# Fill up to 4200 columns a tick, and unread products behind the fill, in a hybrid decoder layer on one core

## The chip, the cores and the metric

The kernel runs on one core of one Trainium2 chip. The metric is the device time of one execution in microseconds (us). Below, PE is TensorE's matmul side and PEld its weight load, DVE is VectorE, ACT is ScalarE, POOL is GpSimd and SP is SyncE, which here issues most of the DMAs.

## The reference, cut to what matters

One layer of a decoder with two SwiGLU blocks and, between them, four mixers that read one combined projection. It is computed for 1024 prompt tokens and for 8 x 4 sample tokens; both go through the projections together, as 1056 columns.

```
h = x + 0.5 * rms_norm(swiglu(rms_norm(x, ng[0]), ...), ng[1])
cols = rms_norm(h, ng[2]) @ p['w_in']
c_gla, c_gmlp, c_rwkv, c_dil = split_at(cols, [GLA_COLS, GMLP_COLS, RWKV_COLS, DIL_COLS])
...
mix = jnp.concatenate([o_gla, o_gmlp, o_rwkv, o_dil], axis=-1) @ p['w_out']
h = h + rms_norm(mix, ng[3])
h = h + 0.5 * rms_norm(swiglu(rms_norm(h, ng[4]), ...), ng[5])
```

The mixers are gated linear attention (gla), a spatial gating (gmlp), RWKV-7 (rwkv) and dilated attention with three groups (dil). Their outputs are long chains of small products and elementwise steps. The products with `w_in`, `w_out` and the SwiGLU weights are large.

## The kernel before, in words

**Large products.** A matrix and its input are each split into two parts of type fp32r, and three products (high times high, high times low, low times high) replace one fp32 product. A product with `w_in` writes a tile `pw` of 128 x 352 (lines 139, 142 and 143, eight times for one tile). The products of the first half of `w_out` (channels of gmlp, rwkv: K3) write `pz`, 128 x 256 (line 2897), and a copy on ScalarE (line 2911) takes each `pz` to the sum `z`. The second half of `w_out` (gla and dil: K4) needs the last mixers; its products (line 204) open what is called the head here: the end of the layer's middle and the start of the second SwiGLU.

**Weights.** `load(j)` brings 512 KB of weights by a DMA of SP (`wraw`), `part(j)` splits them with a cast on ScalarE (line 111, `whi`) and a subtraction on GpSimd (line 112, `wlo`). Both calls stand inside the fill below, so they move with it.

**Two kinds of work in one order.** The program is recorded once, and within it a class `Loom` decides in which order steps are recorded. An engine runs its instructions in that order. The *fill* is one generator, `line()`: the rest of the first SwiGLU, the products with `w_in`, those of K3, a mark `"end"`, and behind `L.mixed == 3` the head. The *streams* are generators of the mixers with priorities. A step runs up to a `yield`. `Loom` keeps rough clocks of all engines from costs of its own (`cost`, `note`), among them the time at which TensorE is free, `free[pe]`, and the columns that went through TensorE (`flow`; `ticks` by stretches of 3.4133 us on that rough clock).

**The rule.** `run` records a step of the fill whenever TensorE is thought to have had little to do, and a step of a stream otherwise:

```
return now > TICK and (sum(n for _, n in self.flow) < WARM or self.ticks.get(k - 1, 0) < FULL)
...
if others and self.cool() and self.weft():
    continue
```

`cool` (line 1446) holds when fewer than `WARM` = 3000 columns lie in the last 3.4133 us of the rough clock, or fewer than `FULL` = 3060 in the last whole stretch. `weft` (line 1531) records one step of the fill: six products of `pw`, or six of `pz`. It returns False when the fill waits for something or is used up. If no stream can go on either, the rough clock is moved ahead.

**The stages that matter below.** The rwkv mixer and gmlp come first, then gla and dil run side by side (dil's attention: lines 2065, 2096, 2107; its merge of the groups: line 2206; its sample tokens: lines 2313 to 2358, with the cached values `cv` loaded by 36 DMAs; gla: lines 2514 to 2616). After the mixers, `mixes01` loads gla's output again (`mx`) and splits it, and only then is `L.mixed` set to 3, which lets the fill go on with the head. From `"end"` to there the fill has nothing to give.

Of the kernel before, what the change touches and what calls it, by code (L numbers as in the profile page):

```python
# [11 lines left out]
F32 = mybir.dt.float32  # L12
# [16 lines left out]
NF = 22  # L29
DF = (0,)  # L30
AGE = 3.
WARM = 3000
I2 = 10.
V, S, G = "vector", "scalar", "gpsimd"
KA = (V, G)
# [15 lines left out]
class Layer:  # L51
    def __init__(self, ctx, tc, I, O):
        self.ctx, self.tc, self.nc = ctx, tc, tc.nc
        self.I, self.O = I, O
        self.pace = Pace()
        self.room = {}
        self.const = ctx.enter_context(tc.tile_pool(name="const", bufs=1))
# [908 lines left out]
class Pace:  # L966
# [11 lines left out]
    def run(self, h):  # L978
        try:
            h[0] = max(h[0], self.clock) + (next(h[1]) or 0.0)  # L980
        except StopIteration:
            h[1] = None
            self.tasks.remove(h)
# [415 lines left out]
class Loom:  # L1399
# [4 lines left out]
    def __init__(self, tc, fill):  # L1404
        self.tc, self.ins = tc, tc.nc.cur_bb.bb.instructions
        self.i, self.last = len(self.ins), {}
        self.free, self.wrote, self.used, self.slots, self.red = {}, {}, {}, {}, {}
        self.fill, self.done, self.over = fill, {}, False
        self.live, self.hold, self.due = [], None, 0.0
        self.fresh, self.marks = [], []  # L1410
        self.ticks, self.flow, self.cells = {}, [], [0.0] * 16
        self.pe = tc.nc.tensor.engine
        self.kept = ()

    def keep(self, engines):

        self.kept = [getattr(self.tc.nc, e).engine for e in engines]
# [27 lines left out]
    def cool(self):  # L1445
# [4 lines left out]
        k = int(now / TICK)  # L1450
        return now > TICK and (sum(n for _, n in self.flow) < WARM or self.ticks.get(k - 1, 0) < FULL)

# [62 lines left out]
    def after(self, gen, prio):  # L1515

        self.fresh.append(self.add(gen, prio))
# [12 lines left out]
    def weft(self):  # L1530
# [13 lines left out]
        self.done[v] = self.late  # L1544
        return True

    def got(self, names):

        return all(self.done.get(n, 1e9) <= self.free.get(self.pe, 0.0) for n in names)
# [24 lines left out]
    def run(self, until, others=True):  # L1574

        while not until():
            now = self.free.get(self.pe, 0.0)
            if others and self.cool() and self.weft():
                continue
            ok = [s for s in self.live if others and self.open(s, now)]  # L1580
            go = [s for s in ok if s[2] <= now + SLACK]
            if go:
                self.step(min(go, key=lambda s: s[0] - (now - s[2]) / AGE))
            elif not self.weft():
                self.free[self.pe] = min(t for t in [self.due] + [s[2] for s in ok] + list(self.done.values()) if t > now)
                self.cells = [max(t, self.free[self.pe]) for t in self.cells]

    def all(self, streams):
        self.run(lambda: all(s[1] is None for s in streams))
# [296 lines left out]
def last_rows(L, ap, raw):  # L1886

    nc, O = L.nc, L.O
    yield lambda: L.loom.got(RW)
    last = ap.tile([128, 8, 33], F32, name="last", tag="mV")  # L1890
    L.dma(last, raw[:, :, TP - 1:T].rearrange("j p t -> p j t"))
    yield
    for jh in range(2):
        rows = ap.tile([33, 512], F32, name="lrows", tag="mvn")
        q = L.ps.tile([128, 512], F32, name="pm", tag="pt", bufs=L.pbufs["pt"])
        for j in range(4):
            nc.tensor.transpose(q[:33, j * 128:(j + 1) * 128], last[:, jh * 4 + j], L.ident)
        nc.scalar.copy(rows, q[:33, :])
        js = slice(jh * 512, (jh + 1) * 512)
        L.put(O["p_shift"][0][:, js], rows[0:1])  # L1900
        L.put(O["s_shift"][0][:, js], rows[4:33:4])
        yield
# [846 lines left out]
def tile_layer(ctx, tc, I, O):  # L2749
    nc = tc.nc  # L2750
    L = Layer(ctx, tc, I, O)
    L.setup()

    def pool(name, side="right", **kw):
        return tc.tile_pool(name=name, bufs=1, side=side, reuse_waits="tile", **kw)
# [36 lines left out]
    nn, no = len(names), len(W_ORDER[0])  # L2792
# [9 lines left out]
    R, W, inside = {}, {}, [0]  # L2802
    L.mixed = -1

    def load(j):
        R[j] = L.raw(*seq[j])

    def part(j):
        if j not in W:
            W[j] = L.parts(R.pop(j), w3 if j in (nn - 3, nn, nn + 4) else None)  # L2810
# [10 lines left out]
    def line():  # L2821
# [116 lines left out]
        yield from ffn2.head("3")  # L2938
        yield "head"

    def weights(js, raws, after):

        for i in range(raws):
            load(js[i])
            L.loom.mark(("raw", js[i]))
            yield 0.0
        for i, j in enumerate(js):
            yield lambda: L.loom.got([("raw", j), after(i)])
            part(j)
            L.loom.mark(("w", j))  # L2950
            yield
            if i + raws < len(js):
                load(js[i + raws])
                L.loom.mark(("raw", js[i + raws]))
                yield 0.0

    def mixes(ks, t):

        for a in (ks[:2], ks[2:]):
            ms = {}  # L2960
            for k in a:
                ms[k] = L.mx.tile([128, TH], F32, name="mx", tag="mx", bufs=2)
                nc.sync.dma_start(ms[k], mixd[k][:, third(t)])
            yield
            for k in a:
                L.split(xs3[k][0][:, third(t)], xs3[k][1][:, third(t)], ms[k])
            yield

    def mixes01():
        yield lambda: L.loom.got(["end"]) and gls[1][1] is None  # L2970
        for t in range(NTH):
            yield from mixes((0, 1), t)
# [3 lines left out]
    with pool("sp1") as L.sp, pool("hid1") as hp, pool("ps1", space=PSUM) as L.ps:  # L2976
# [93 lines left out]
        loom = L.loom = Loom(tc, line())  # L3070
        loom.keep(KA)
        loom.add(weights(range(no + 2), 2, lambda i: ("1", "w", i) if i < 4 else ("o", 2, i - 4)), -0.7)
        for u, i in enumerate(ORDER):
            loom.add(L.follow(ffn1.y, i, "1", L.res, h1_d, lambda u: hp.tile([128, D], F32, name="hn", tag="h%d" % (10 + u)), (xs2, 2)), -2.5 + u / 100)
# [3 lines left out]
    with pool("mxp") as L.mx, pool("ps2", space=PSUM) as L.ps:  # L3078
        L.pbufs = {"pt": 1, "pa": 3, "py": 2}
        L.mixed = 0  # L3080
        loom.keep(KR2)
        with pool("gm") as gp, pool("rwc") as cp:
            gm = loom.add(chain(gmlp(L, gp, cold, mixd), last_rows(L, gp, raw)), 3)
            C = {}
            rc = loom.add(rwkv_consts(L, cp, C), 2)
            loom.run(lambda: set(loom.done) >= set(RW) and rc[1] is None)
            wx.close()
            loom.keep(KR)
            with pool("rwp") as rp:
                rwkv(L, C, rp, raw, mixd)  # L3090
            loom.all([gm])
            L.mixed = 2
        loom.keep(KM)
        w3 = ctx.enter_context(pool("w3", "left"))
        L.room[w3] = 1
        with pool("gla") as ap:
            gls = [loom.add(x, GP) for x in gla(L, ap, cold, mixd)]
            m01 = loom.add(mixes01(), 4)
            dil(L, pool, lambda n, t: L.dma(t, cold[n]), xs3)
            loom.all([*gls, m01])  # L3100
    stx.close()


# [37 lines left out]
    loom = L.loom = Loom(tc, ffn2.tail("2"))  # L3141
# [38 lines left out]
```

## Time and profile before

| | |
|---|---|
| median of 3 runs | 2499.03 us (2498.38 to 2510.2) |
| the profiled execution's own time | 2503.86 us |
| its span in the trace | 2502.1 us |
| TensorE busy | 2411.0 us, 96% |
| VectorE, ScalarE, GpSimd busy | 1395.5, 1013.6, 1067.8 us |
| mean granted TensorE clock | 0.972 |
| fill ends (last `pz` product) | 1630.5 us |
| first product of the head (line 204, behind the mixers) | 1680.69 us |

Times in the trace count from the span's start; 1.8 us lie outside of the span. A busy share of TensorE is time in which some product was under way, whatever its size; the clock is what the profile's rows call PEclk, 1.00 for full speed. A line number can be that of a helper that many places call.

### The profile page before, as it was taken

The numbers are of one execution on the slowest core, as the hardware profiler recorded it, in microseconds if no ns is written. First come the engines' busy times: TensorE is split into PE (matmuls) and PEld (weight loads), VectorE is DVE, ScalarE is ACT, GpSimd is POOL, SyncE is SP. The second block draws the span as 40 slices with busy tenths as digits, with TensorE's granted clock in tenths as the row PEclk, the third lists the DMA queues.
The fourth block names the chain that finished last, engine by engine and source line by source line (L and its number), as shares of the span: only waits on it lengthen the run. The fifth ranks groups of instructions, "written<-read, shape, count | busy, mean of one in ns | idle before, by whom it ended". The sixth has DMA issues, their size and how long they took to land. (4 is left out here: it accounts for less than half of the span.)

```text
span 2502.1 us, 41009 instructions
## 1 busy us (share of the span) xinstructions
PE 2411.0 (96%) x15543; PEld 2207.7 (88%) x15543; DVE 1395.5 (56%) x3211; ACT 1013.6 (41%) x2175; POOL 1067.8 (43%) x902
## 2 busy tenths in 40 slices
PE   8999999999999999999999999968999999999997
PEld 8999999977789998898888899737989999997777
DVE  7645454367775056665632467437854444447767
ACT  5433333366554242323324344415533333336651
POOL 3655555567643233232111111114355555557664
PEclk9999999999999999999989889969999999999999
DMA  4322222323434333231226676444222222233334
GB/s 133 100 69 83 66 82 68 106 86 111 119 126 132 93 106 90 87 100 52 74 56 195 185 228 184 134 130 146 79 86 74 80 74 80 72 103 92 104 103 148
DMA packets 273612, 265.21 MB, mean 106 GB/s; under 512 B 36283, under 2 KB 247380, under 8 KB 273414
## 3 DMA queue, kind: packets, MB, share of 16 engines
q1 hardware_dynamic: 223810, 212.69, 28.9%
q10 hardware_dynamic: 49604, 49.90, 5.8%
q8 instruction: 122, 2.00, 0.3%
q14 instruction: 76, 0.62, 0.1%
HBM read 195.26 MB, written 67.16 MB: 105 GB/s over the span
## 5 line engine op out<-in xcount | busy, mean ns | idle before, releaser
L520 POOL TENSOR_TENSOR wlo<-wraw,whi 128x512 fp32r<-128x512 f32 x280 | 379.7, 1374 | 355.1 <-ACT whi L519 355.0
L549 PE MATMUL p<-xh,whi 128*128 128x352 f32 x1120 | 364.0, 325 | 5.4 <-DVE hid L475 3.6
L551 PE MATMUL p<-xh,wlo 128*128 128x352 f32 x1120 | 362.3, 323 | 0.0
L550 PE MATMUL p<-xl,whi 128*128 128x352 f32 x1120 | 361.2, 322 | 0.0
L519 ACT CAST whi<-wraw 128x512 fp32r<-128x512 f32 x280 | 166.5, 620 | 409.1 <-PE p L550 293.4
L112 POOL TENSOR_TENSOR wlo<-wraw,whi 128x1024 fp32r<-128x1024 f32 x61 | 146.0, 2396 | 391.8 <-ACT whi L111 343.6
L139 PE MATMUL pw<-xh,whi 128*128 128x352 f32 x888 | 308.1, 347 | 2.3 <-ACT stg L2782 1.5
L143 PE MATMUL pw<-xh,wlo 128*128 128x352 f32 x888 | 293.4, 330 | 0.0
L142 PE MATMUL pw<-xl,whi 128*128 128x352 f32 x888 | 293.1, 330 | 0.0
L549 PEld LDWEIGHTS p<-xh,whi 128*128 128x128 f32 x1120 | 211.4, 189 | 6.8 <-DVE hid L475 3.9
L550 PEld LDWEIGHTS p<-xl,whi 128*128 128x128 f32 x1120 | 211.5, 189 | 0.0
L551 PEld LDWEIGHTS p<-xh,wlo 128*128 128x128 f32 x1120 | 210.4, 188 | 0.0
L139 PEld LDWEIGHTS pw<-xh,whi 128*128 128x128 f32 x888 | 171.5, 193 | 13.3 <-issue 7.5
L142 PEld LDWEIGHTS pw<-xl,whi 128*128 128x128 f32 x888 | 172.1, 194 | 1.9 <-issue 1.7
L143 PEld LDWEIGHTS pw<-xh,wlo 128*128 128x128 f32 x888 | 171.2, 193 | 1.4 <-issue 1.2
L549 PE MATMUL p<-hid,whi 128*128 128x352 f32 x400 | 129.9, 325 | 1.8 <-ACT n L583 1.4
L551 PE MATMUL p<-hid,wlo 128*128 128x352 f32 x400 | 129.8, 324 | 1.4 <-POOL wlo L520 1.4
L550 PE MATMUL p<-hid,whi 128*128 128x352 f32 x400 | 129.2, 323 | 0.0
L111 ACT CAST whi<-wraw 128x1024 fp32r<-128x1024 f32 x61 | 63.9, 1048 | 118.7 <-PE pw L142 85.2
L723 PE MATMUL p<-xh,hid 128*128 128x512 f32 x320 | 109.8, 397 | 0.1
L204 PE MATMUL pt<-whi,ya 128*128 128x256 f32 x512 | 97.7, 290 | 1.0 <-POOL ya L793 1.0
L839 DVE TENSOR_TENSOR y<-y,p 128x512 f32<-128x512 f32 x112 | 76.6, 685 | 38.7 <-PE p L723 36.7
(641 smaller groups left out, 5861.9 us busy)
## 6 DMA issues: line engine op xcount, KB each, us to landing
wraw<-in_w_ff_gate_dram SPq DMA_DIRECT2D x44, 512.0 KB
wraw<-in_w_ff_up_dram SPq DMA_DIRECT2D x44, 512.0 KB
wraw<-in_w_in_dram SPq DMA_DIRECT2D x37, 512.0 KB
wraw<-in_w_ff_down_dram SPq DMA_DIRECT2D x36, 512.0 KB
hid_d<-tmp ACTq DMA_DIRECT2D x60, 176.0 KB
hid_d<-n ACTq DMA_DIRECT2D x60, 176.0 KB
cv<-in_cache_win_dram SPq DMA_DIRECT2D x36, 256.0 KB
whi<-hid_d SPq DMA_DIRECT2D x32, 256.0 KB
```

Of the source, the lines that this page charges most:

```text
L112: nc.gpsimd.tensor_tensor(lo, raw, hi.bitcast(F32), op=OP.subtract)
L139: ins = nc.tensor.matmul(out, a, xh[:, cs], start=(first and i == 0), stop=False)
L142: nc.tensor.matmul(out, a, xl[:, cs], start=False, stop=False)
L143: nc.tensor.matmul(out, b, xh[:, cs], start=False, stop=(last and i == n - 1))
L204: nc.tensor.matmul(out, xs[kx][a][:, cs], ws[js[0]][b][:, kw], start=u == a == b == 0, stop=u == len(kk) - 1 and a == 1, skip_group_check= ...
L519: nc.scalar.copy(t[0][:, i], v)
L520: nc.gpsimd.tensor_tensor(t[1][:, i], v, t[0][:, i].bitcast(F32), op=OP.subtract)
L549: nc.tensor.matmul(out, ah, xh, start=first and k == 0, stop=False, skip_group_check=True)
L550: nc.tensor.matmul(out, ah, xl, start=False, stop=False, skip_group_check=True)
L551: nc.tensor.matmul(out, al, xh, start=False, stop=k == KH - 1, skip_group_check=True)
L723: nc.tensor.matmul(out, a[i][:, u], b[j][:, u], start=first and u == i == j == 0, stop=u == n - 1 and i == 1, skip_group_check=True)
L839: (nc.vector.tensor_copy if h else nc.scalar.copy)(v, p) if copy else nc.vector.tensor_add(v, v, p)
```

## The change

Two things change. `WARM` goes from 3000 to 4200, everywhere that `Loom` decides. And while gla and dil run, `Loom` has a second resort: once `"end"` is recorded, `turn` records four products of a weight tile with itself into a PSUM tile `pk` that nobody reads, whenever `cool` holds and the fill gives nothing.

```diff
-WARM = 3000
+WARM = 4200
...
+    def turn(self):
+        if not self.spare or not self.spare():
+            return False
+        i, prev = len(self.ins), self.last.get(self.pe)
+        self.spin()
+        if prev:
+            self.tc.add_manual_dep(self.ins[i], prev, mybir.DependencyInfo(
+                mybir.DependencyClass.NoSync, mybir.DependencyReason.DATA), reason="order")
+        self.reckon()
+        return True
...
-            if others and self.cool() and self.weft():
+            if others and self.cool() and (self.weft() or self.turn()):
                 continue
...
+    def spin():
+        p = L.ps.tile([128, 256], F32, name="pk", tag="pw", bufs=2)
+        w = W[nn + 4][0]
+        for u in range(4):
+            nc.tensor.matmul(p, w[:, u, :128], w[:, u], start=True, stop=True)
...
             gls = [loom.add(x, GP) for x in gla(L, ap, cold, mixd)]
+            loom.spare, loom.spin = lambda: "end" in loom.done, spin
             m01 = loom.add(mixes01(), 4)
             dil(L, pool, lambda n, t: L.dma(t, cold[n]), xs3)
             loom.all([*gls, m01])
+            loom.spare = None
```

The added code moves line numbers: in the changed kernel 1306 stays, 1849 is 1863, 2065 is 2079, 2206 is 2220, 2347 is 2361, 2589 is 2603, 2616 is 2630, 2897 is 2911, and the unread products are line 2959.

Counted over the whole order, TensorE gets 388 products more (97 calls of `spin`), all `pk`; every other kind of instruction is there as often as before, on every engine, and SP issues 739 DMAs in both. TensorE's order is the same up to the rwkv mixer (the first row that differs ran at 905.5 us) and again from within the second SwiGLU. In between the fill's products stand earlier among those of the streams. At the point of the order where the changed kernel's last `pz` stands, 345 products of the mixers are still to come; in the kernel before, 86 are left at its last `pz`. Before that point (the mixers' product that ran at 1555.55 us) 192 fill products more are done than before.

The first place is TensorE in the rwkv mixer, around the 16 products of the sample tokens that write 8 columns each (`rws`, line 1849, then 1863). Before:

```order
L1837 MATMUL pm<-work 64x32 x2
L1306 MATMUL pm<-rgl,g_7856 128x256
L1819 MATMUL pm<-tri 32x32 x2
L1841 MATMUL pm<-ident,work 128x32
L1306 MATMUL pm<-rgl,g_7856 128x256
L139 MATMUL pw<-xh,whi 128x352
L1849 MATMUL pm<-rws,S_12571 64x8 x16
L1824 MATMUL pm<-UVs,work 32x64 x2
L142 MATMUL pw<-xl,whi 128x352
```

The same place in the changed kernel:

```order
L1855 MATMUL pm<-ident,work 128x32
L1827 MATMUL pm<-tri,work 32x32 x2
L139 MATMUL pw<-xh,whi 128x352
L142 MATMUL pw<-xl,whi 128x352
L143 MATMUL pw<-xh,wlo 128x352
L139 MATMUL pw<-xh,whi 128x352
L142 MATMUL pw<-xl,whi 128x352
L143 MATMUL pw<-xh,wlo 128x352
L1863 MATMUL pm<-rws,S_12655 64x8 x16
L1833 MATMUL pm<-tri 32x32 x2
L139 MATMUL pw<-xh,whi 128x352
```

One fill product stood between the small ones before; now six stand directly ahead of the 16 and more fill follows two small products behind them.

The second place is TensorE among the scores of dil's attention (`qT`, `kT`; line 2065, then 2079), at 1388 us of the trace before. Before:

```order
L2065 MATMUL pm<-kT,qT 128x128 x2
L139 MATMUL pw<-xh,whi 128x352
L142 MATMUL pw<-xl,whi 128x352
L143 MATMUL pw<-xh,wlo 128x352
L139 MATMUL pw<-xh,whi 128x352
L2065 MATMUL pm<-kT,qT 128x128 x2
L142 MATMUL pw<-xl,whi 128x352
L143 MATMUL pw<-xh,wlo 128x352
L139 MATMUL pw<-xh,whi 128x352
L2065 MATMUL pm<-kT,qT 128x128 x2
L142 MATMUL pw<-xl,whi 128x352
L2065 MATMUL pm<-kT,qT 128x128 x4
```

The same place in the changed kernel:

```order
L2079 MATMUL pm<-kT,qT 128x128 x2
L139 MATMUL pw<-xh,whi 128x352
L142 MATMUL pw<-xl,whi 128x352
L143 MATMUL pw<-xh,wlo 128x352
L2079 MATMUL pm<-kT,qT 128x128 x2
L139 MATMUL pw<-xh,whi 128x352
L142 MATMUL pw<-xl,whi 128x352
L143 MATMUL pw<-xh,wlo 128x352
L2079 MATMUL pm<-kT,qT 128x128 x2
L139 MATMUL pw<-xh,whi 128x352
L2079 MATMUL pm<-kT,qT 128x128 x4
```

Between these scores hardly anything moved: four, three and one fill products before, three, three and one now.

The third place is TensorE at the end of the mixers: the last merges of dil (`on`, line 2206, then 2220), gla's last sample products (`gex`, `gsp`), and the head's first product (`pt`, line 204). Before:

```order
L2589 MATMUL pm<-gex,gkn 32x512 x4
L2206 MATMUL pm<-ident,on 128x128 x2
L2616 MATMUL pm<-ident,gsp 128x32 x2
L2206 MATMUL pm<-ident,on 128x128 x2
L204 MATMUL pt<-whi,xl 128x256
```

The same place in the changed kernel:

```order
L2603 MATMUL pm<-gex,gkn 32x512
L2959 MATMUL pk<-whi 128x256 x20
L2220 MATMUL pm<-ident,on 128x128 x2
L2959 MATMUL pk<-whi 128x256 x24
L2630 MATMUL pm<-ident,gsp 128x32 x2
L2959 MATMUL pk<-whi 128x256 x8
L2220 MATMUL pm<-ident,on 128x128 x2
L2959 MATMUL pk<-whi 128x256 x68
L204 MATMUL pt<-whi,xl 128x256
```

Unread products now stand between each of these steps, and 68 of them behind the last merge, ahead of the head's first product.

More of the change, by code (lines that the diff above doesn't have):

```diff
@@ L1413, in __init__ @@
         self.kept = ()
+        self.spare = self.spin = None
     def keep(self, engines):
```

## The prediction

> **What bounds the kernel now.** I read the page first, then the stretches between the order's first change (905.5 us) and the head (1680.69 us), cut where the granted clock changes, then TensorE's order of time ahead of one such cut, then who TensorE waits for at the mixers' end.
>
> From the page, TensorE's share and the rows of 40 slices (62.6 us each) for its busy tenths and clock:
>
> ```profile
> PE 2411.0 (96%) x15543; PEld 2207.7 (88%) x15543; DVE 1395.5 (56%) x3211; ACT 1013.6 (41%) x2175; POOL 1067.8 (43%) x902
> PE   8999999999999999999999999968999999999997
> PEclk9999999999999999999989889969999999999999
> ```
>
> Only TensorE is near its limit, and its clock falls from the 21st to the 27th slice: the stage that the change reorders. The same stage by stretches (length, then busy time and instructions by engine, granted clock, DMA):
>
> ```profile
> core 0: us, PE busy (x) PEld busy (x) DVE busy (x) ACT busy (x) POOL busy (x), PEclk, DMA share, GB/s
> 905.50:1555.55 650.05, 636.42 (x4615) 573.05 (x4614) 361.87 (x1175) 229.65 (x601) 132.74 (x135) 0.95 0.41 123
> 1283.82:1287.24 3.42, 3.42 (x45) 2.69 (x41) 1.09 (x3) 0.78 (x4) 0.00 (x0) 1.00 0.17 62
> 1287.24:1307.72 20.48, 20.48 (x102) 15.59 (x101) 3.51 (x8) 3.25 (x13) 0.00 (x0) 0.50 0.09 26
> 1389.64:1406.70 17.06, 17.06 (x69) 13.65 (x69) 4.76 (x29) 6.47 (x29) 0.45 (x2) 0.50 0.30 88
> 1430.60:1437.42 6.82, 6.82 (x26) 5.61 (x26) 2.46 (x20) 0.29 (x1) 0.00 (x0) 0.50 0.80 223
> 1457.90:1471.56 13.66, 13.66 (x58) 11.98 (x58) 7.87 (x21) 3.54 (x12) 0.45 (x2) 0.50 0.82 251
> 1481.80:1485.21 3.41, 3.41 (x13) 3.19 (x12) 1.16 (x12) 1.38 (x4) 0.61 (x1) 0.50 0.95 261
> 1555.55:1630.47 74.92, 73.37 (x637) 58.18 (x636) 37.18 (x130) 30.91 (x89) 13.48 (x13) 1.00 0.45 136
> 1630.47:1680.69 50.22, 32.55 (x159) 14.32 (x158) 21.12 (x76) 9.45 (x26) 5.64 (x8) 0.65 0.40 121
> 1649.05:1686.60 37.55, 23.77 (x97) 13.07 (x97) 17.82 (x52) 6.95 (x20) 7.57 (x8) 0.50 0.25 71
> 1680.69:1840.00 159.31, 139.49 (x952) 133.81 (x951) 119.97 (x345) 81.94 (x194) 63.75 (x41) 0.93 0.35 114
> ```
>
> Up to 1630.47 us TensorE idles for 650.05 - 636.42 = 13.6 us and then 1.6 us: its products follow each other without a hole, and what is added to its order is added to the time. In five spells it runs at half clock, always busy: 20.48 + 17.06 + 6.82 + 13.66 + 3.41 = 61.4 us, half of it lost, 30.7 us. That is the most a fuller order can win back there. Behind the fill's end TensorE is idle for 50.22 - 32.55 = 17.7 us, at half clock for most of the rest.
>
> Ahead of the first spell (start, length, engine, line, tiles, active rows and columns, shape, records; an fp32 product makes two records):
>
> ```profile
> 1283.60 0.30 PE L1837 MATMUL pm<-work 32*64 32x32 f32 x4
> 1283.83 0.70 PE L1306 MATMUL pm<-rgl,g 128*128 128x256 f32 x2
> 1284.46 0.31 PE L1819 MATMUL pm<-tri 32*32 32x32 f32 x4
> 1284.70 0.24 PE L1841 MATMUL pm<-ident,work 32*128 32x32 f32 x1
> 1284.87 0.70 PE L1306 MATMUL pm<-rgl,g 128*128 128x256 f32 x2
> 1285.22 0.51 PE L139 MATMUL pw<-xh,whi 128*128 128x352 f32 x1
> 1285.66 1.92 PE L1849 MATMUL pm<-rws,S 64*64 64x8 f32 x32
> ```
>
> TensorE is busy for all 3.42 us before the clock falls, but with little: 1024 columns of line 1306, 352 of the fill, 256 of 8 columns each and some 300 of 32, about 1900. For comparison a stretch of the head in which large products stand back to back:
>
> ```profile
> 1703.00:1717.00 14.00, 14.00 (x120) 14.00 (x119) 12.03 (x30) 5.33 (x13) 8.43 (x6) 1.00 0.44 147
> ```
>
> There 120 products of 256 columns take 14.00 us: 0.117 us each, some 7500 columns in 3.42 us. I take it that the clock falls for want of columns, a quarter of the full flow in that stretch, not for want of busy time. The Trainium skill ("TensorE: Matmul & The Clock Gate", "HAM oscillation") has as its rule that TensorE keeps its clock as long as no idle gap exceeds about 3.4 us. By that rule neither this spell nor the change's denser fill would mean anything; the trace has a spell behind 3.42 busy us of 3.42, so here the row decides against it, and the rule returns as a rival.
>
> **The change part by part.** The sum is made against the profiled execution (2503.86 us, 4.8 above the median of 2499.03), and its difference is then put on the median.
>
> *Unread products.* 388 of 128 x 256 at 0.117 us are 45.3 us of TensorE. They write tiles of the fill's own tag, which has two buffers: only the first two calls wait for ScalarE, for the last copies of `pz`, and the later ones for TensorE's own products of two calls before. From the page's groups (busy us, mean ns of one):
>
> ```profile
> L204 PE MATMUL pt<-whi,ya 128*128 128x256 f32 x512 | 97.7, 290 | 1.0 <-POOL ya L793 1.0
> ```
>
> A product of this shape is over 290 ns after it starts, and four of 117 ns lie between, so that wait holds nothing up. What they displace is counted below: as much of them as falls into idle time costs nothing. If nothing hid them, all 45.3 us would be on the path, since every later product stands behind them.
>
> *Fill put earlier.* It adds no work. The 192 products that now stand before the point of 1555.55 us delay it by 192 x 0.117 = 22.4 us, and the stretch from there to 1630.47 us loses them; counted in the order, 176 unread products take their place there. So this shift cancels in the sum, except that the fill is used up sooner, which the 45.3 us pay for. The weight loads, the casts on ScalarE and the subtractions on GpSimd move along, past dil's and rwkv's own DMAs on SP; ScalarE is busy for 229.65 and GpSimd for 132.74 of 650.05 us, and this covers them. If SP's queue held a load back, TensorE would wait at a fill product; the waits up to 1630 us are too small in all for me to price that above 5 us.
>
> *Half clock regained, 1287 to 1485 us.* At the first spell six full products now stand right ahead of the small ones and more behind them, 2112 columns where 352 stood: I call it gone. Ahead of the third, the order has 18 fill products of 256 columns among the scores that had five of 352 (4608 columns for 1760): gone. At the second the rows hardly differ, so it stays. At the last two the fill is by then `pz` with 256 columns and no denser than before in places: I take half. Gone are 20.48 + 6.82 + (13.66 + 3.41)/2 = 35.8 us of half clock, worth 17.9 us. The bounds are 0 (all remain, or others replace them) and 30.7.
>
> *Idle time before the fill's end.* 13.6 + 1.6 us, waits for VectorE and ScalarE within streams. A denser fill covers some: 3 us, between 0 and 8.
>
> *The mixers' end.* What TensorE waits for between 1630.47 and 1681 us (us in total, times, longest), and then, from the order of time, one step of gla at full and at half clock:
>
> ```profile
> PE pm L2206 <- DVE rst L1017: 4.1, 1, 4.1
> PE pm L2589 <- DVE gex L2583: 3.2, 1, 3.2
> PE pm L2347 <- DMA cv<-in_cache_win_dram: 2.5, 5, 0.7
> PE pm L2616 <- DVE gsp L2610: 2.5, 1, 2.5
> ```
>
> ```profile
> 1647.26 1.97 PE L2576 MATMUL pgo<-gq,gSF 128*128 128x4 f32 x16
> 1654.09 3.58 PE L2576 MATMUL pgo<-gq,gSF 128*128 128x4 f32 x16
> ```
>
> The last two are the same products: the clock is worth a factor of 1.82 even with 4 columns. The 23.77 busy us from 1649.05 to 1686.60, at half clock throughout, would take 23.77/1.82 = 13.1 us with the clock kept up by the unread products: 10.7 us less, the last few of them in the head's first products. The bounds are 0 (the clock falls there all the same) and 11.9 (half). The unread products stand just where TensorE waits: 20 (2.3 us) ahead of the wait of 4.1, 24 (2.8 us) ahead of that of 2.5, 1 to 24 among the `cv` products. I let them fill 9 of the 17.7 idle us; the bounds are 0 and 17.7. The last 68 (7.9 us) find no such wait, since the head's first product followed the last merge at once; they are on the path in full.
>
> *The head.* Its order changes too (products of line 204 against the steps of the norm behind them), with the same work. It idles for 159.31 - 139.49 = 19.8 us and its mean clock is 0.93, so it can move either way, by 4 us as I guess from a fifth of that idle time. I take 0.
>
> *Sum.* 45.3 - 17.9 - 3 - 10.7 - 9 + 0 = +4.7 us: 2508.6 for a profiled execution, **2503.7 us** on the median, no change within 0.5% (12.5 us, about what a measurement of this kernel can tell from no change).
>
> **The rivals.**
>
> *Faster.* All five spells go (12.8 us more than I take), and the unread products fall wholly into the 17.7 idle us at the end (8.7 more): 2503.7 - 12.8 - 8.7 = 2482 us. For it speaks that the target rises by 1200 columns, a sixth of the full flow of 7500. Against it: the second spell's rows are the same, and the 68 at the end stand ahead of nothing that waits.
>
> *Slower.* The clock does not come back: what rules it is not the flow that `Loom` counts, or the rough clock is so far from the chip's that new spells open where fill has been taken away. Then the 17.9 us stay lost and the unread products still cost: 2503.7 + 17.9 = 2521.6 us. It decides once over 41 of the 61.4 us of half clock remain: then at most 10.1 us are regained where I take 17.9, and the sum passes 12.5. This is also the time that follows from the skill's rule of idle gaps (same page and section), since without such gaps there would be nothing to regain. For it speaks that `Loom` gave at least 3000 columns by its own count where the trace shows about 1900. Against it speaks the first place in the order.
>
> *The change does not do what it says*: the clock falls at the mixers' end all the same, because the calls of `spin` are planned by the rough clock and leave holes where the chip is slow. The 10.7 us are then not saved: 2514.4 us. The order has a run of 15 products of `cv` there without an unread one. I count it with the slower cases.
>
> **How the numbers follow.** Forecast (within 12.5 us) 0.54; the faster rival 0.24; the two slower ones 0.22 together, 0.16 and 0.06. The range 2482 to 2518 leaves out about one in ten on each side: its lower end is the faster rival with nothing from the head, its upper end lies just under the case where no clock returns. Faster 0.24, same 0.54, slower 0.22.
>
> **What would show it.** In the changed profile: the clock at 1.00 where the 16 small products of the sample tokens run, and again among the scores ahead of the third spell; a spell still to be seen among the scores at the second; the last `pz` near 1630.5 - 75 + 22.4 - 20.9, that is 1557 us, and the head's first product near 1685; the 388 `pk` at 0.117 us; the clock at 1.00 from the fill's end to the head. The prediction is wrong if the head's first product comes before 1672 or after 1697 us, and its reason is wrong if the spells go and it still isn't earlier at the fill's end, or if they stay.

## The result, and the profile after

The changed kernel takes 2532.34 us (median of four runs, 2526.27 to 2534.54), the kernel before 2499.47 us beside it. The ratio is 1.0129, 95% interval [1.0102, 1.0156]: slower by 33 us, beyond the range that the forecast gave (2482 to 2518 us). The profiled execution is the fastest of the four, 2526.27 us, and that of before lay 4 us above its median, so the two traces differ by only 22.4 us.

TensorE's share and the rows of 40 slices (63.1 us each) on the page of the changed kernel:

```profile
PE 2445.1 (97%) x15931; PEld 2249.8 (89%) x15931; DVE 1401.0 (55%) x3211; ACT 1013.1 (40%) x2175; POOL 1069.4 (42%) x902
PE   8999999999999999999999999988999999999997
PEclk9999999999999999999999888999999999999998
```

TensorE is busier (2445.1 us for 2411.0) and its clock is better: the 6 in the slice at the mixers' end is gone. Both are what the change is made of, and the time is longer. The stretches that answer to those of before: up to the last `pz`, the stretches ahead of and within two spells of half clock, the last `pz` to the head's first product, and as much of the head as was shown of before:

```profile
core 0: us, PE busy (x) PEld busy (x) DVE busy (x) ACT busy (x) POOL busy (x), PEclk, DMA share, GB/s
905.50:1580.66 675.16, 657.46 (x4803) 595.59 (x4802) 370.62 (x1171) 234.32 (x609) 138.74 (x137) 0.96 0.40 119
1292.37:1295.78 3.41, 3.41 (x45) 3.00 (x45) 0.39 (x2) 0.71 (x5) 0.00 (x0) 1.00 0.18 58
1295.78:1306.02 10.24, 10.24 (x35) 7.34 (x35) 3.04 (x6) 0.94 (x4) 0.00 (x0) 0.50 0.00 0
1534.72:1538.13 3.41, 0.77 (x7) 0.76 (x7) 3.06 (x12) 0.29 (x1) 0.00 (x0) 1.00 0.83 253
1538.13:1551.79 13.66, 13.66 (x62) 11.64 (x61) 8.90 (x37) 1.98 (x8) 0.00 (x0) 0.50 0.43 146
1580.66:1713.77 133.11, 124.45 (x986) 95.29 (x985) 60.35 (x212) 34.92 (x106) 15.64 (x19) 0.97 0.43 131
1713.77:1873.08 159.31, 145.36 (x1025) 141.25 (x1024) 121.77 (x347) 84.24 (x198) 67.52 (x43) 0.97 0.33 110
```

The last `pz` runs at 1580.66 us, 49.8 us earlier than before, and the head begins at 1713.77, 33.1 us later. Between the two lie 133.11 us instead of 50.22. The clock there is 0.97, held up by the unread products, whose rows among the groups of the whole run and, at 65 of them back to back right ahead of the head, among the stretches are:

```profile
L2959 PE MATMUL pk<-whi 128*128 128x256 f32 x388 | 56.8, 299 | 0.0
```

```profile
1705.90:1713.30 7.40, 7.40 (x65) 7.40 (x64) 3.34 (x4) 0.78 (x2) 1.65 (x1) 1.00 0.63 206
```

7.40 us over 65 is 0.114 us each, as forecast (0.117).

A way to split the 33.1 us: before, the 259 mixers' products between the two fill ends (345 - 86) ran beside fill from 1555.55 to 1630.47 us, 74.92 us, of which 192 fill products took 22.4 us; so they cost 52.5 us in company, as an estimate that charges the fill products at 0.117 us each. Now they stand behind the fill.

- Ahead of the fill's end one expects 650.05 + 22.4 = 672.5 us if nothing else changes, and 675.2 are measured: 2.7 us lost where the forecast won 20.9.
- Behind it one expects 50.2 + 52.5 = 102.7 us without the unread products, and 133.1 are measured: 30.4 us lost where the forecast lost 25.3.
- From the head's first product to the end, 810.8 us for 821.4: 10.6 us won, where the forecast had nothing.

The spells of half clock ahead of the fill's end, from the granted clock: before 20.5, 17.1, 6.8, 13.7 and 3.4 us, 61.4 in all; now 10.2 (at 1295.8), 3.4 (1367.5), 13.7 (1401.6), 10.2 (1449.4), 3.4 (1490.3), 3.4 (1500.6) and 13.7 (1538.1), 58.0 in all. What TensorE does ahead of the first of them, the place of the 16 small products of the sample tokens:

```profile
1291.78 1.82 PE L1863 MATMUL pm<-rws,S 64*64 64x8 f32 x32
1293.53 0.31 PE L1833 MATMUL pm<-tri 32*32 32x32 f32 x4
1293.77 0.43 PE L139 MATMUL pw<-xh,whi 128*128 128x352 f32 x1
1294.04 0.32 PE L142 MATMUL pw<-xl,whi 128*128 128x352 f32 x1
1294.19 0.32 PE L143 MATMUL pw<-xh,wlo 128*128 128x352 f32 x1
1294.35 0.32 PE L139 MATMUL pw<-xh,whi 128*128 128x352 f32 x1
1294.51 0.32 PE L142 MATMUL pw<-xl,whi 128*128 128x352 f32 x1
1294.67 0.32 PE L143 MATMUL pw<-xh,wlo 128*128 128x352 f32 x1
1294.92 0.30 PE L1870 MATMUL pm<-work,UVs 64*64 64x32 f32 x4
1295.15 0.41 PE L1838 MATMUL pm<-UVs,work 32*32 32x64 f32 x4
1295.49 0.29 PE L1874 MATMUL pm<-ident,rws 128*32 128x128 f32 x1
1295.53 0.44 PE L139 MATMUL pw<-xh,whi 128*128 128x352 f32 x1
```

In the 3.41 us ahead of the spell stand seven fill products now, where one stood before: some 3300 columns, counted as the prediction counted its 1900. The clock falls all the same.

TensorE's longest waits up to the fill's end and, from the order of time, what stands ahead of the last spell:

```profile
PE pm L2450 <- ACT Vn L2040: 2.6, 2, 2.1
PE pm L2079 <- DVE gSS L2533: 2.6, 1, 2.6
PE pz L2911 <- ACT z L2925: 2.5, 2, 1.4
```

```profile
1534.45 0.28 PE L2911 MATMUL pz<-whi,xl 128*128 128x256 f32 x1
1537.37 1.20 PE L2079 MATMUL pm<-kT,qT 64*128 64x128 f32 x7 [2.64 <-DVE gSS L2533]
```

So two different stretches precede a spell. From 1292.37 TensorE is busy for all 3.41 us, with small products and seven large ones; from 1534.72 it waits 2.64 us for VectorE behind the last product of a fill step. The second place had no spell before. By the rule that the prediction weighed (the Trainium skill, "TensorE: Matmul & The Clock Gate", "HAM oscillation": no idle gap over about 3.4 us) neither should cost the clock. The trace disagrees with it again, with 0 and 2.64 us of waiting.

### The profile page after: what moved, and what is told of

The parts are those of the page before. It is cut to its first block, busy times and chain, and to the rows that moved or that the text cites. A ratio compares the mean times of both kernels' runs of the same rounds, so it can differ in the third digit from the quotient of the medians.

```text
span 2524.5 us, 41805 instructions
## 1 busy us (share of the span) xinstructions
PE 2445.1 (97%) x15931; PEld 2249.8 (89%) x15931; DVE 1401.0 (55%) x3211; ACT 1013.1 (40%) x2175; POOL 1069.4 (42%) x902
## 5 line engine op out<-in xcount | busy, mean ns | idle before, releaser
L139 PEld LDWEIGHTS pw<-xh,whi 128*128 128x128 f32 x888 | 169.2, 191 | 10.7 <-issue 6.2
L204 PE MATMUL pt<-whi,ya 128*128 128x256 f32 x512 | 99.5, 293 | 1.3 <-POOL ya L793 1.3
```

What stands on the lines that cost most here:

```text
L139: ins = nc.tensor.matmul(out, a, xh[:, cs], start=(first and i == 0), stop=False)
L204: nc.tensor.matmul(out, xs[kx][a][:, cs], ws[js[0]][b][:, kw], start=u == a == b == 0, stop=u == len(kk) - 1 and a == 1, skip_group_check= ...
```

## The experiments

Three theories stood at the start. A: the earlier fill wins back no clock and is used up sooner, and the unread products only pay for the clock that the mixers' end then lacks. B: the unread products are ballast. C: it is the limit of 4200 and the places it picks. Each kernel was timed beside the kernel before, whose medians lay between 2498.03 and 2500.51 us. One execution differs from another of the same kernel by up to 28 us, so a trace's own time is given where it is read.

All of them in one table. "Left" counts the mixers' products that stand behind the last `pz` in the order; half clock is that between 905 us and the fill's end, in the one profiled execution; "tail" is from there to the head's first product.

| kernel | limits | unread | left | half clock, us | fill's end, us | tail, us | median, us | ratio |
|---|---|---|---|---|---|---|---|---|
| before | 3000 | 0 | 86 | 61.4 | 1630.5 | 50.2 | 2499.5 | 1 |
| changed | 4200 | 388 | 345 | 58.0 | 1580.7 | 133.1 | 2532.3 | 1.0129 [1.0102, 1.0156] |
| e1 | 4200 | 0 | 345 | 78.5 | 1592.9 | 122.3 | 2532.0 | 1.0136 [1.0106, 1.0166] |
| e2 | 3000 | 144 | 86 | 37.5 | 1620.2 | 58.9 | 2514.2 | 1.0057 [1.0038, 1.0076] |
| e3 | 4200 | 328 | 345 | 71.7 | 1587.5 | 125.2 | 2532.5 | 1.0124 [1.0098, 1.0150] |
| e4 | 3000, then 4200 | 396 | 345 | 41.0 | 1579.2 | 143.8 | 2537.8 | 1.0151 [1.0126, 1.0175] |
| e5 | 3000, head 4200 | 0 | 86 | 54.6 | 1631.7 | 49.7 | 2499.1 | 0.9998 [0.9982, 1.0014] |
| e6 | 3600 | 0 | 245 | 60.9 | 1604.6 | 99.3 | 2521.4 | 1.0096 [1.0065, 1.0126] |
| e7 | 2400 | 0 | 21 | 122.9 | 1693.5 | 9.9 | 2516.5 | 1.0070 [1.0047, 1.0094] |
| e8 | 4200 | 148 | 345 | 61.4 | 1586.3 | 130.0 | 2538.4 | 1.0152 [1.0123, 1.0180] |
| e9 | 4200, then 3000 | 0 | 259 | 47.8 | 1604.3 | 99.5 | 2519.8 | 1.0083 [1.0057, 1.0108] |
| e10 | 3600, then 3000 | 0 | 81 | 63.3 | 1644.7 | 48.7 | 2519.0 | 1.0083 [1.0050, 1.0116] |
| e11 | 3000, then 2400 | 0 | 58 | 68.3 | 1654.2 | 37.5 | 2502.9 | 1.0021 [1.0001, 1.0041] |
| e12 | 2400, then 3000 | 0 | 17 | 112.6 | 1697.7 | 9.3 | 2532.2 | 1.0147 [1.0120, 1.0175] |
| e13 | 3000, truer clock | 0 | 294 | 105.8 | 1621.7 | 110.3 | 2549.9 | 1.0202 [1.0175, 1.0230] |
| e14 | 2000 and 2560, truer clock | 0 | 105 | 150.2 | 1676.2 | 55.2 | 2552.4 | 1.0230 [1.0198, 1.0263] |
| e15 | 3000 and FULL 2560 | 0 | 59 | 54.6 | 1644.0 | 34.8 | 2493.7 | 0.9982 [0.9967, 0.9998] |

**The limit alone (e1).**

```diff
-            if others and self.cool() and (self.weft() or self.turn()):
+            if others and self.cool() and self.weft():
```

> The limit of 4200 stays and the 388 unread products go, so the order up to the last `pz` is that of the changed kernel. Theory A (the earlier fill wins back no clock, is used up some 50 us sooner, and the unread products pay with their own 45.3 us for the clock that they hold up behind it): the 345 mixers' products left behind the fill fall to half clock for most of the 87.8 us (133.1 less 45.3) that they take at full clock, so little or nothing is won: 2520 to 2535 us. Theory B (the unread products are simply ballast, the mixers' products keep the clock without them): 45 us less, 2487 to 2495 us.

Measured: 2531.95 us, as the changed kernel. Theory B falls: with no unread product at all the loss is the same. The stretches up to the fill's end, from there to the head, and the head:

```profile
905.50:1592.90 687.40, 670.04 (x4825) 607.29 (x4823) 370.09 (x1176) 237.16 (x615) 140.13 (x137) 0.94 0.40 118
1592.90:1715.20 122.30, 95.80 (x598) 59.91 (x597) 59.79 (x209) 33.88 (x104) 16.14 (x19) 0.75 0.44 133
1715.20:1874.51 159.31, 142.10 (x981) 136.74 (x980) 118.42 (x346) 81.72 (x195) 63.14 (x40) 0.94 0.36 114
```

Left to themselves the mixers' products leave TensorE idle for 122.30 - 95.80 = 26.5 us, at a clock of 0.75, and take 122.3 us where the two stretches of before give 50.2 + 52.5 = 102.7. Ahead of the fill's end 687.4 us stand against 672.5 expected, with the order of the changed kernel. 14.9 and 19.6 us make the 34.5 by which the head is late. Up to the fill's end e1 and the changed kernel have one order, so the 12.2 us between them there (687.4 for 675.2) are a difference of executions, most of it the clock: 20.5 us more of half clock are worth 10.2. The unread products of the changed kernel lengthen the tail of e1 to 133.1 us, by 10.8: of their 45.3 us they give back 34.5.

**The unread products alone (e2).**

```diff
-WARM = 4200
+WARM = 3000
```

> The limit is 3000 again and the unread products stay; with the later fill there are 144 of them (16.8 us) and 86 mixers' products behind the fill. Theory A: they save some 10.7 us of half clock and fall partly into idle time, 2495 to 2506 us, no change against before. Theory B (each unread product costs as in the changed kernel, 33 us over 388): 12 us more than before, 2511 us.

Measured: 2514.16 us (2500.95 to 2517.96), 14 us over before, near the 16.8 us that the 144 products take and nearer to B's 2511 than to A's range, which ended at 2506. With the limit of 3000, then, the unread products are mostly ballast, as B has it. Its trace is of the fastest of nine runs:

```profile
905.50:1620.20 714.70, 698.98 (x5234) 622.48 (x5232) 398.81 (x1300) 258.76 (x682) 146.77 (x147) 0.97 0.42 126
1620.20:1679.10 58.90, 49.25 (x302) 30.88 (x301) 22.54 (x79) 10.33 (x28) 8.27 (x9) 0.91 0.37 112
```

The tail's clock rises from 0.65 to 0.91 and its idle time falls from 17.7 to 9.65 us, and it is 8.7 us longer all the same: the products gave back 8.1 of 16.8 us there. The other 5 us of the median's 14 no trace shows. The stretch ahead has the order of before to the last product, and took 10.3 us less, with 37.5 us of half clock for 61.4. So one order gives different sums of half clock from one execution to the next.

The places are steadier than the sums. Up to the fill's end the kernel before, e2 and e5 have one order, and the changed kernel, e1, e3 and e8 the other, so their spells can be set side by side by the place in TensorE's order (named by the time in the first of each group), in us of half clock:

| order of before, place | before | e2 | e5 |
|---|---|---|---|
| 1287, the 16 small products | 20.5 | 0 | 20.5 |
| 1390, dil's scores | 17.1 | 13.7 | 10.2 |
| 1431 | 6.8 | 6.8 | 3.4 |
| 1458 | 13.7 | 13.7 | 13.7 |
| elsewhere | 3.4 | 3.4 | 6.8 |

| order of the changed kernel, place | changed | e1 | e3 | e8 |
|---|---|---|---|---|
| 1296, the 16 small products | 10.2 | 13.7 | 13.7 | 13.7 |
| 1359 to 1372 | 3.4 | 6.8 | 6.8 | 6.8 |
| 1402, dil's scores | 13.7 | 13.7 | 10.2 | 13.7 |
| 1449 to 1472 | 10.2 | 10.2 | 6.8 | 10.2 |
| 1490 to 1504 | 6.8 | 17.1 | 17.1 | 3.4 |
| 1538 | 13.7 | 17.1 | 17.1 | 13.7 |

Most spells come back at their place in every execution; what varies is their length, by one or a few times 3.4 us, and at one place (1287 in e2) a whole spell of 20.5 us is missing. The places 1296, 1402 and 1449 lie at the mixers' products of 1287, 1390 and 1431 before; at those of 1458 the spell is gone, and those of 1538 had none. Ahead of 1538 TensorE's wait for VectorE stands in all four traces of the changed order (2.62 to 2.74 us).

**Fewer unread products (e3 and e8).** e3 gives them up before the last stream is run out, e8 gives them only below 2000 columns:

```diff
+            loom.spare = None
             loom.all([*gls, m01])
-            loom.spare = None
```

```diff
-        if not self.spare or not self.spare():
+        if not self.spare or not self.spare() or sum(n for _, n in self.flow) >= 2000:
```

> The changed kernel with unread products only until dil is recorded to its end: 328 instead of 388, 8 instead of 68 right ahead of the head. If the 60 stand on the path and hold nothing up, 60 x 0.117 = 7.0 us less than the changed kernel, some 2525 us. If they keep the clock up for the head's start, no less: 2530 to 2534 us, with half clock at the head's first products.

> The changed kernel with an unread step only when fewer than 2000 columns stand in the rough clock's last tick: 148 unread products (17.3 us) for 388 (45.3 us), the fill and its order as in the changed kernel. If the unread products cost what they take, 20 to 28 us less, 2505 to 2512 us. If each of them only takes the place of half clock or of waiting (with none at all the kernel took 2532 us), no change against the changed kernel, 2525 to 2537 us.

Measured: 2532.49 and 2538.42 us. With 0, 148, 328 and 388 unread products the time is 2532.0, 2538.4, 2532.5 and 2532.3: their number does not matter, within the 6 us by which e8 stands apart and the 6 to 7 us that the intervals leave open for each. The tail of e3, with 328:

```profile
1587.50:1712.70 125.20, 116.78 (x926) 86.56 (x924) 57.93 (x209) 34.94 (x106) 14.87 (x19) 0.97 0.42 127
```

The tail of e8, with 148:

```profile
1586.30:1716.30 130.00, 112.84 (x746) 75.55 (x745) 61.73 (x210) 34.93 (x106) 16.03 (x19) 0.83 0.40 122
```

Fewer than half as many keep the clock at 0.83 and leave 17.2 us idle; many keep it at 0.97 and leave 8.4. What one has in clock the other has in products that nobody reads. e3's 60 products fewer (7.0 us) shorten the tail in the trace (125.2 for 133.1) but bring nothing to the median that its interval could tell. The time is that of its second case, but the sign named there is not seen: the clock stays up for 38 us behind the head's first product, and then 17.1 us of half clock come in the first 160 us for 10.2 in the changed kernel.

**Where the limit acts (e4 and e9).** `cool` reads a limit that changes where gla and dil start; in e4 from 3000 to 4200, with the unread products, in e9 from 4200 to 3000, without. The line that sets it, in e4 and then in e9:

```diff
-        return now > TICK and (sum(n for _, n in self.flow) < WARM or ...
+        return now > TICK and (sum(n for _, n in self.flow) < self.warm or ...
...
         loom.keep(KM)
+        loom.warm = 4200
```

```diff
             gls = [loom.add(x, GP) for x in gla(L, ap, cold, mixd)]
+            loom.warm = 3000
```

> The limit is 4200 only from where gla and dil start, 3000 during rwkv and gmlp and again nothing else is changed: 396 unread products, 345 mixers' products behind the fill. If what counts is how much fill is left for dil and gla (theory A), it goes as the changed kernel, 2527 to 2537 us. If the places in the rwkv mixer where fill was put in or taken away cost the time, it lies 5 us or more below, under 2525 us.

> The other half of the limit alone: 4200 up to where gla and dil start, 3000 from there, no unread products. 259 mixers' products are left behind the fill (86 in the kernel before, 345 with 4200 throughout). Theory A (the time goes with what the used-up fill leaves behind): 32 us x (259 - 86) / (345 - 86) = 21 us over before, 2515 to 2527 us. Theory D (4200 hurts only where gla and dil run, as the run with it there alone was as slow as the changed kernel): as before, 2495 to 2504 us.

Measured: 2537.84 and 2519.76 us. The late half does it all, as A has it, but the early half costs 22 us by itself, so it is not that only the late stage is touchy (theory D of e9's expectation falls). What both have in common is the mixers' products that are left, and e9 came out at the 21 us that the count gave. Both had less half clock ahead of the fill's end than before (41.0 and 47.8 us for 61.4, in one execution each) and were slower even so, with tails of 143.8 and 99.5 us.

**Other limits (e5, e6, e7, e10, e11, e12).** e6 and e7 set `WARM` to 3600 and to 2400; e10, e11 and e12 change it where gla and dil start, as in e9; e5 sets 4200 only behind the last mixer:

```diff
             loom.all([*gls, m01])
+            loom.warm = 4200
```

> The kernel before up to the head, with the limit 4200 only from the head on and no unread products. In the changed kernel the stretch from the head's first product to the end was 10.6 us shorter than before (810.8 for 821.4 us). If that comes from the head's own order under the limit of 4200, this kernel is 5 to 10 us faster than before, 2490 to 2495 us. If it comes from the unread products that stand right ahead of the head and start it at full clock, it is as before, 2500 us.

> Limit 3600, no unread products; 245 mixers' products are left behind the fill (86 at 3000, 345 at 4200). Theory A (the time goes with the mixers' products that the used-up fill leaves behind): between the two, 32 us x (245 - 86) / (345 - 86) = 20 us over before, 2512 to 2525 us. Theory C (a limit of 4200 spoils the places within the fill): about as before, 2497 to 2506 us, or anything that does not follow this count.

> Limit 2400, no unread products; 21 mixers' products are left behind the fill. Theory A: 32 us x (86 - 21) / (345 - 86) = 8 us less than before by that term, if the thinner fill does not add half clock ahead of its end; 2490 to 2500 us. If the thinner fill lets the clock fall more often among the streams, as the idea of the change has it, slower than before: 2505 to 2520 us.

> 3600 up to where gla and dil start, then 3000, no unread products; 81 mixers' products are left behind the fill, nearly as many as before (86). Theory A: as before, 2495 to 2504 us. Theory D also. If the denser fill among rwkv's products keeps the clock up there, as the idea of the change has it, up to 10 us faster: 2488 to 2495 us.

> 3000 up to where gla and dil start, then 2400, no unread products; 58 mixers' products left behind the fill. By their count alone (theory A) 32 us x (86 - 58) / (345 - 86) = 3.5 us less than before, 2492 to 2500 us. If what made the run with 2400 throughout 18 us slower is half clock among gla's and dil's products, 2505 to 2515 us.

> 2400 up to where gla and dil start, then 3000, no unread products; 17 mixers' products left behind the fill. By their count alone (theory A) 32 us x (86 - 17) / (345 - 86) = 8.5 us less than before, 2487 to 2495 us. If the thinner fill among rwkv's products lets the clock fall there (with 2400 throughout, three spells of 14 us together stood ahead of 1200 us, where before had none), slower than before: 2505 to 2515 us.

Measured: e5 2499.13 us, as before, so the limit in the head is worth nothing. e6 2521.38 us, 23 over its own runs of before, as the count of products left has it (20). e7 2516.5, e10 2518.97, e11 2502.86 and e12 2532.2 us: here theory A in its simple form, time by the count of what is left, fails four times; they have fewer left than before and are slower (e11 by 5 us, just clear of its interval). For e7 and e12 the stretches up to the fill's end and from there to the head show why. First e7 (2400 throughout):

```profile
905.50:1693.50 788.00, 760.98 (x5351) 664.15 (x5350) 412.11 (x1370) 264.17 (x699) 151.62 (x155) 0.92 0.40 120
1693.50:1703.40 9.90, 7.47 (x41) 2.36 (x39) 5.56 (x8) 2.76 (x6) 2.76 (x2) 1.00 0.81 252
```

The same of e12 (2400, then 3000):

```profile
905.50:1697.70 792.20, 760.78 (x5361) 663.66 (x5360) 404.17 (x1350) 262.71 (x696) 150.84 (x153) 0.93 0.40 121
1697.70:1707.00 9.30, 5.76 (x27) 2.05 (x26) 5.53 (x20) 4.81 (x13) 0.23 (x1) 0.83 0.13 28
```

The tail has all but gone, but ahead of the fill's end TensorE idles for 27.0 and 31.4 us (before 15.2), with 122.9 and 112.6 us of half clock (61.4). So the limit has a loss on each side: too low, and the clock falls beside the streams; too high, and the fill is gone when the last streams need it. e10 fits neither: 19.1 us idle, 63.3 us of half clock and a tail of 48.7, all close to before, and its head starts 12.6 us late in the trace. Of that, 3.4 us lie ahead of the first product whose place differs (at 927.71 us before, 931.13 in e10), so the limit has no part in them. From there to the head it is 3.7 us more idle time and, with 11.9 us less half clock, some 11.5 us more busy time for the same products, which no view of the profile names. Of the theories only C leaves room for it, without saying which place it is.

**A truer rough clock (e13, e14), and FULL (e15).** If 4200 wins back no clock because the rough clock does not see the lulls, one closer to the chip should. e13 raises its costs to the trace's; e14 lowers the limits too:

```diff
-LAT = 0.14
+LAT = 0.2
...
-                return (max(n / 2.4, m / 1.2) + 2) / 1e3
+                return (max(n / 2.19, m / 1.2) + 2) / 1e3
...
-            return (n + 100) / 960
+            return (n + 190) / 960
...
-            return (2 * n + 100) / 960
-        return 0.09 + n / 1200 + 0.19 * (len(x.outs) > 1)
+            return (2 * n + 250) / 960
+        return 0.155 + n / 1200 + 0.19 * (len(x.outs) > 1)
```

e15 is the kernel before with `FULL` at 2560 for 3060.

> The kernel before with the same limit of 3000 and a rough clock nearer to the chip's: costs per instruction raised to what the trace shows (0.117 us for a product of 256 columns, some 0.06 to 0.16 us more for an operation of VectorE, ScalarE or GpSimd, 0.2 us for 0.14 from one engine to the next). 294 mixers' products are left behind the fill, between 3600's 245 and 4200's 345. Theory E (the limit of 4200 wins back no clock because the rough clock runs ahead of the chip's and does not see the lulls): the half clock ahead of the fill's end falls from some 60 us to under 40 us, though the tail still costs some 25 us more than before: 2505 to 2520 us. If the lulls do not hang on the rough clock, some 60 us of half clock remain and the time is that of the limits 3600 to 4200, 2520 to 2535 us.

> The truer rough clock with lower limits (2000 for WARM, 2560 for FULL), so that 105 mixers' products are left behind the fill, near the 86 of the kernel before. Theory E: the half clock ahead of the fill's end is no more than before, with the same tail: 2485 to 2500 us. If the lulls do not hang on the rough clock: the limits are lower, the clock falls more often, as with 2400: 2510 to 2525 us.

> The kernel before with its second limit, FULL, at 2560 for 3060 and WARM at 3000: 59 mixers' products are left behind the fill. It tells whether the order before is special: if the time hangs on the balance of fill and tail alone, it is as before, 2495 to 2508 us; if nearly any other order costs some 20 us, as 3600 and then 3000 did with 81 left, 2512 to 2525 us.

Measured: 2549.85 and 2552.35 us, with 105.8 and 150.2 us of half clock ahead of the fill's end. Theory E falls, at least for costs that are truer on average: the spells grow, and these orders are the slowest of all. e15 takes 2493.71 us, 0.9982 [0.9967, 0.9998] of before: it has fewer products left (59) and less half clock (54.6 us) than before, the only kernel with both, and is 4 us faster, just clear of its interval. So not every other order is slower. e13's stretches up to the fill's end and in the tail, where both losses come together:

```profile
905.50:1621.70 716.20, 688.87 (x4922) 620.28 (x4921) 383.34 (x1239) 240.29 (x635) 146.38 (x149) 0.93 0.40 119
1621.70:1732.00 110.30, 89.58 (x517) 51.44 (x516) 41.82 (x158) 29.26 (x89) 11.57 (x18) 0.73 0.37 113
```

## Why the prediction was wrong, point by point

- **What bounds the kernel** held: TensorE, without holes up to the fill's end, and half clock in the stage that the change reorders.
- **Half clock regained, -17.9 us**: this step failed, and it is the larger part of the miss in the trace. 58.0 of 61.4 us remained, worth 1.7 us, so 16.2 us did not come back; the three other executions of the same order had 61.4, 71.7 and 78.5. The forecast called a spell gone where the order has more columns now. At the first place, on which it relied most, six or seven fill products stand in the 3.41 us ahead of the spell for one, 2600 to 3300 columns for 1900, and 10.2 to 13.7 us of half clock are there in all four executions, where the order before had 20.5 in two of three. At the second the spell stays, as forecast. At the third, called gone, or just behind it stand 6.8 to 10.2 us for 3.4 to 6.8. The fourth is gone and the last has 3.4 to 17.1 us, but a new one of 13.7 to 17.1 us stands at 1538 us in all four, behind a wait of 2.6 to 2.7 us that the traces of the order before do not have. As 3300 columns are still below half of the full flow of 7500 that the prediction counts, a want of columns is not ruled out as the reason; shown is that these additions were not enough.
- **Idle time ahead of the fill's end, -3 us**: this failed too. 17.7 us of it stand there, for 13.6 before up to the same point of the order: 4.1 more where 3 less were forecast, 7.1 us of miss. With the 16.2 us of clock this makes 23.3 of the 23.7 us by which the last `pz` came later than the forecast 1557 us.
- **Unread products**: 388 at 0.114 to 0.117 us, as forecast, and in the tail they and the earlier fill cost 30.4 us where the sum had 45.3 - 10.7 - 9 = 25.6. That size is nearly right, but the reason is wrong, and with it **the step "this shift cancels in the sum", except "that the fill is used up sooner, which the 45.3 us pay for"**. In e1 nothing pays for it, and the kernel is as slow: 259 mixers' products that cost 52.5 us beside the fill cost 72.1 without it (122.3 - 50.2), and nothing was won ahead of the fill's end. Against that tail the unread products give back 34.5 of their 45.3 us. They are one way to pay this bill, half clock and waiting the other, and the medians put both at 31 to 33 us.
- **The clock at the mixers' end** came back, as forecast (0.97 up to the head, with two spells of 3.4 us); the rival by which the change does not do what it says is out.
- **The tail** took 133.1 us, where the marks 1557 and 1685 made 128: 5.1 us more.
- **The head** took 10.6 us less, where I had put 0. The sum is 4.7 + 23.7 + 5.1 - 10.6 = 22.9 for the measured 22.4 us. Its limit does nothing (e5). From the head's first product to the end the traces show 810.8 us in the changed kernel, 821.4 before and 812.1 to 822.5 in the fifteen experiments, with 812.1 in e11, which has no unread product. It goes with the half clock in the head's first 160 us: 10.2 us in the changed kernel and 23.0 before, worth 6.4 of the 10.6 us; the five traces with the shortest rest (810.8 to 814.6 us) have 10.2 to 16.1 us of it, the six with the longest (819.3 to 822.5) 17.1 to 30.9. Whether the change brings this or the two traces caught two ends of what one execution differs from another is open; the medians lie 33 us apart, not 22.4, and without the 10.6 us the terms add up to 33.5.
- **The rivals**: "Slower: the clock does not come back" is what happened. Its point of decision, over 41 of 61.4 us remaining, was passed with 58.0. It had a chance of 0.16 and a time of 2521.6 us, 11 us below the measured; it left out the 7.1 us of idle time and the 5.1 us of the tail.

Open is what decides where and for how long the clock falls, and why e10 is slower than before. Shown is that neither 4200 columns throughout by the rough clock's count (58.0 to 78.5 us in four executions) nor the truer rough clock (105.8 and 150.2) lowers the half clock ahead of the fill's end, which is 37.5 to 61.4 us in three executions of the order before.

## What to carry to other kernels

Work that is put in to fill lulls is a stock: given out faster, it runs out sooner, and what it covered then stands bare; so cost the stretch behind its end by the same products run in company and alone, before costing anything that is to replace it. Products that nobody reads can hold the clock, but here they took as much time as they gave back, or more. And a spell of half clock is not gone because a few large products were put ahead of it: look at its place in several executions of both orders before counting it as a gain, and look for new spells where work was taken away.

## What the hardware showed that was not expected

One order of instructions had between 37.5 and 61.4 us of half clock in three executions, another between 58.0 and 78.5 in four. Most spells stood at the same places each time, in lengths of one to six times 3.4 us; one of 20.5 us was missing in one execution. Single times of one kernel lay up to 28 us apart (2504.52 to 2532.43 in e10). The clock fell both behind 3.41 us in which TensorE was busy throughout, with seven large products among the small ones, and behind a wait of 2.64 us.
